# A diffusion layer on one core: the values' copies out of PSUM placed behind a weight block's split, and a small transpose one step of products later

## The chip, the core and the metric

The kernel runs on one core of one Trainium2 chip. The metric is the device time of one execution in microseconds (us); the number given for a kernel is the median of its runs. Five engines run side by side, each through its own queue and in the order of that queue: TensorE (PE in the profile, with its weight loads as PEld), VectorE (DVE), ScalarE (ACT), GpSimd (POOL) and SyncE (SP), which here issues the DMA transfers. Semaphores order the engines against each other.

## The reference

One layer of a diffusion backbone in float32, with 256 latent tokens, 256 context tokens and 2048 channels. Both kinds of token are normed and modulated (a scale and a shift that come from a conditioning vector, different for latent and context tokens). The result h is multiplied by one large matrix for queries, keys, values and gates:

```
h  = rms_norm(x, g) * (1 + scale)   + shift
hc = rms_norm(ctx, g) * (1 + scale_c) + shift_c
qa, ka, va, qb, kb, vb, ga, gb = split(h @ w_in)
```

Two attentions follow (a windowed one with 8 query heads and 2 key heads, and one over a neighbourhood with 8 heads; both also see the context), then gates, two branch matrices, an output matrix, and a gated feed-forward part with a short convolution. The values that this case is about are va and vb: 512 tokens by 10 heads of 128 channels, 1280 columns in all.

## The kernel before

**Numbers and splits.** Float32 products are made of two parts: each operand is split into a high part and the rest (names ending in h and l), and each product is three matmuls: high by high, low by high, high by low. A weight block of 128 x 2048 numbers is loaded by SyncE into one of four buffers called `raw`; ScalarE writes its high part `wh` (line 144) and VectorE the rest `wl` (line 148), in two halves of 1024 columns each. There are two buffers of `wh` and two of `wl`, so a block can be split when TensorE has read the block two before it for the last time.

**The stages.** By the first and last start of their matmuls in the trace: modulation and keys (`pk`) to 148.8 us, the values (`pv`) from 149.1 to 264.8, queries and attention (`pq`) to 426.6, gates and branches (`pg`, `pb`) to 677.8, the output matrix (`py_o`) to 764.7, the feed-forward matrix up (`pu`) to 1261.5 and down (`c`, `x`) to 1490.4.

**The values.** Lines 738 to 765 compute them in three column groups: 512, 512 and 256 columns wide, with 4, 4 and 2 weight blocks. The document counts these blocks from 0 to 9 (`nb` in the code): 0 to 3 are group 0, 4 to 7 group 1, 8 and 9 group 2; block 10 is the first one of the queries. A group accumulates in four PSUM banks, one for each 128 tokens (`pv0_0` to `pv0_3` for group 0 and so on). Six banks take turns for such sums: group 2's first two are free for a long time when it begins, its third and fourth are those of group 1's first and second. When a group's products are through, ScalarE copies the four banks into `vv` (line 765).

A block is walked in steps (`kk`): four steps for a wide group, eight for the narrow one, with four token tiles of three matmuls in each. The call `block(2)` at a block's beginning asks for the split of the next block and for the load of the one after it. `last` holds the two instructions of the latest split; `last[0]` is ScalarE's.

**What goes on beside them.** The keys were multiplied before the shift was known, so what the shift adds is computed during the value products. `late_dots` and `shift_done` (lines 675 to 693) finish the shift on VectorE and add it to the last channels of h. `shift_rows` (line 695) subtracts the two shifts (line 696, into `rim`), transposes the columns of the shift to rows on TensorE (`ptsd`, line 698), copies them out on ScalarE (line 700), sends them to memory and brings them back spread over all partitions (`shr`, lines 701 to 704). `beside` (line 718) then lets VectorE take one dot product of 2048 columns (line 726) for each head of keys against that row, out of a `raw` buffer that it loads too; `kb` is the sum, and `key_bias` (line 709) adds it to `kT` on ScalarE (line 712), with a rotation by position (`tr_k`, lines 319 to 322) for the last two heads. While no keys are due, `beside` takes dot products of a later modulation instead (line 247).

**What sets the order.** In this part of the program a scheduler places the instructions of each engine, led by the order of the code and its own estimates. `tc.issue_after(x)` binds the instructions inside it to stand behind x on x's engine. So the code says what must be computed and the scheduler says in which order; the order of instructions that it gives is shown below.

## Time and profile before

| | |
|---|---|
| median of 3 runs | 1501.37 us (1500.74 to 1503.16) |
| the profiled execution | 1499.85 us |
| its span in the profile | 1498.1 us |
| granted clock of TensorE, mean | 0.999 |
| TensorE busy | 1483.5 us (99%) |
| VectorE busy | 1220.7 us (81%) |
| ScalarE busy | 820.0 us (55%) |

The span runs from the first to the last instruction that the profiler saw; the execution's own time has 1.75 us more around it. In a timeline, a row has the start in us from the span's beginning, the duration, the engine, the line, the operation, what it writes and reads, how many instructions the row takes together and, in brackets, how long the engine stood idle before and what ended that. In a list of waits, a row says which instruction waited for which engine's instruction, for how long in total, how many times, and the longest.

### The profile page before, as it was taken

The numbers are of one execution on the slowest core, as the hardware profiler recorded it, in microseconds if no ns is written. First come the engines' busy times: TensorE is split into PE (matmuls) and PEld (weight loads), VectorE is DVE, ScalarE is ACT, GpSimd is POOL, SyncE is SP. The second block draws the span as 40 slices with busy tenths as digits, with TensorE's granted clock in tenths as the row PEclk, the third lists the DMA queues.
The fourth block names the chain that finished last, engine by engine and source line by source line (L and its number), as shares of the span: only waits on it lengthen the run. The fifth ranks groups of instructions, "written<-read, shape, count | busy, mean of one in ns | idle before, by whom it ended". The sixth has DMA issues, their size and how long they took to land.

```text
span 1498.1 us, 21728 instructions
## 1 busy us (share of the span) xinstructions
PE 1483.5 (99%) x8487; PEld 1279.7 (85%) x8487; DVE 1220.7 (81%) x1852; ACT 820.0 (55%) x1361; POOL 1.8 (0%) x11
## 2 busy tenths in 40 slices
PE   9999999999999999999999999999999999999998
PEld 7877888998988888888888888888888888888886
DVE  4499877889988888877778887887888878887887
ACT  5553323677765445555666555555555556445543
POOL 0000000000000000000000000000000000000000
PEclk9999999999999999999999999999999999999999
DMA  9988696764468888878856666666666654655652
GB/s 372 396 320 338 262 399 256 298 213 158 152 225 299 311 320 328 314 273 336 317 201 223 251 231 242 237 240 231 249 222 231 225 186 166 225 219 187 263 216 112
DMA packets 61159, 383.72 MB, mean 256 GB/s; under 512 B 6512, under 2 KB 8960, under 8 KB 18304
## 3 DMA queue, kind: packets, MB, share of 16 engines
q1 hardware_dynamic: 60336, 381.26, 68.1%
q8 instruction: 67, 1.10, 0.3%
q10 hardware_dynamic: 720, 1.07, 0.2%
q14 instruction: 36, 0.29, 0.1%
HBM read 378.05 MB, written 4.25 MB: 255 GB/s over the span
## 4 chain that ended last, share of the span: by engine, by line
PE 95%; DVE 2%; ACT 1%; issue 1%; DMA 1%; POOL 0%; SPq 0%; DVEq 0%; POOLq 0%
PE pu L217 21%; PE c L1368 12%; PE pu L218 11%; PE pg L217 7%; PE pk L498 7%; PE py_o L993 6%; PE pv L760 5%; PE pq L217 4%; PE pb L217 4%; PE pg L218 4%; PE x L1368 3%; PE pq L218 2%; PE pb L218 2%; PE po L901 1%; PE s L870 1%; PE pm L371 1%
## 5 line engine op out<-in xcount | busy, mean ns | idle before, releaser
L148 DVE TENSOR_TENSOR wl<-raw,wh 128x1024 fp32r<-128x1024 f32 (+1 forms) x444 | 521.2, 1202 | 134.4 <-ACT wh L144 133.5
L144 ACT ACTIVATE wh<-raw 128x1024 fp32r<-128x1024 f32 (+1 forms) x444 | 444.6, 1037 | 201.2 <-PE pg L217 54.8
L217 PE MATMUL pu<-h,wh 128*128 128x512 f32 x1404 | 487.6, 391 | 0.0
L218 PE MATMUL pu<-h,wl 128*128 128x256 f32 x1404 | 396.0, 282 | 0.0
L217 PEld LDWEIGHTS pu<-h,wh 128*128 128x128 f32 x1404 | 263.6, 188 | 54.7
L218 PEld LDWEIGHTS pu<-h,wl 128*128 128x128 f32 x1404 | 265.7, 189 | 0.0
L217 PE MATMUL pg<-h,wh 128*128 128x512 f32 x464 | 161.5, 390 | 0.0
L1368 PE MATMUL c<-wh,ff 128*128 128x512 f32 x448 | 138.0, 389 | 0.0
L218 PE MATMUL pg<-h,wl 128*128 128x256 f32 x464 | 130.9, 282 | 0.0
L498 PE MATMUL pk<-h,ku 128*128 128x512 f32 x480 | 117.6, 398 | 0.5 <-DVE h L412 0.3
L222 ACT ACTIVATE half_u<-pu 128x256 f32<-128x256 f32 x88 | 33.5, 383 | 147.9 <-PE pu L218 147.9
L247 DVE SCALAR_TENSOR_TENSOR raw<-raw,crb 128x2048 f32<-128x2048 f32 x48 | 109.6, 2286 | 2.8 <-DMA raw<-in_wm_b_dram 2.8
L217 PE MATMUL pq<-h,wh 128*128 128x512 f32 x304 | 108.8, 396 | 2.3 <-ACT wh L144 2.3
L498 PEld LDWEIGHTS pk<-h,ku 128*128 128x128 f32 x480 | 87.7, 188 | 24.0 <-issue 3.9
L217 PEld LDWEIGHTS pg<-h,wh 128*128 128x128 f32 x464 | 87.1, 188 | 18.1
L760 PE MATMUL pv<-wh,h 128*128 128x512 f32 (+1 forms) x384 | 101.3, 354 | 1.2 <-ACT wh L144 1.2
L1368 PEld LDWEIGHTS c<-wh,ff 128*128 128x128 f32 x448 | 84.1, 188 | 17.4
L217 PE MATMUL pb<-h,wh 128*128 128x512 f32 x256 | 89.4, 391 | 0.0
L218 PEld LDWEIGHTS pg<-h,wl 128*128 128x128 f32 x464 | 87.8, 189 | 0.0
L1368 PE MATMUL c<-wl,ff 128*128 128x512 f32 x224 | 87.4, 390 | 0.0
L218 PE MATMUL pq<-h,wl 128*128 128x256 f32 x304 | 85.6, 282 | 0.0
L993 PE MATMUL py_o<-wh,zz 128*128 128x512 f32 x256 | 78.4, 389 | 0.0
(252 smaller groups left out, 2090.6 us busy)
## 6 DMA issues: line engine op xcount, KB each, us to landing
raw<-in_ws_dram SPq DMA_DIRECT2D x222, 1024.0 KB, 4.9
raw<-in_wm_b_dram SPq DMA_DIRECT2D x64, 1024.0 KB, 4.9
raw<-in_wm_sc_dram SPq DMA_DIRECT2D x15, 1024.0 KB, 8.2
raw<-in_wkt_dram SPq DMA_DIRECT2D x10, 1024.0 KB, 7.5
raw<-in_wm_sh_dram SPq DMA_DIRECT2D x8, 1024.0 KB, 9.3
sd<-in_wm_sd_dram SPq DMA_DIRECT2D x6, 1024.0 KB, 6.2
raw<-in_wk_dram SPq DMA_DIRECT2D x7, 768.0 KB, 8.4
crb<-sild SPq DMA_DIRECT2D x5, 1024.0 KB, 8.7
```

Source lines behind the costliest of these rows:

```text
L144: a_ = nc.scalar.activation(hi, src, AF.Copy)
L148: v_ = nc.vector.tensor_tensor(out=lo, in0=src, in1=hi, op=ALU.subtract)
L217: nc.tensor.matmul(pt[:, :], wh[:, w], a, start=first and i == 0, stop=False, skip_group_check=True)
L218: nc.tensor.matmul(pt[:, :S], wl[:, w], a[:, 0], start=False, stop=last and i == n - 1, skip_group_check=True)
L222: a_ = nc.scalar.activation(t[:], pt[:, S:], AF.Copy)
L247: nc.vector.scalar_tensor_tensor(out=r, in0=r, scalar=1.0, in1=row, op0=ALU.mult, op1=ALU.mult, accum_out=modx[:, j : j + 1])
L371: nc.tensor.matmul(pm[32 * j : 32 * j + 32, t * P : t * P + P], cc[:, q, :], rsc[k + t][:, q * P : q * P + P], start=q < 4, stop=q >= KT - ...
L498: nc.tensor.matmul(pk[:], wt[:, w], hh[:, :, k, a], start=k == 0 and a == 0 and wt is wh, stop=k == KT - 1 and a == 1)
L760: nc.tensor.matmul(pv[i][:, :nw], src[:, k, a, t0 : t0 + P], wt[:, w], start=k == 0 and q == 0, stop=k == KT - 1 and q == 2)
L870: nc.tensor.matmul(s_ps, qs[hd][:, a, qt * P : qt * P + P], k_[:, w], start=q == 0, stop=q == 2)
L993: p_ = nc.tensor.matmul(py[t][:], act[:, k, a, t * P : t * P + P], wt[:, w], start=k == 0 and q == 0, stop=k == nk - 1 and q == 2)
L1368: nc.tensor.matmul(pt[:], a(i), wt[:, w], start=k not in begun, stop=stop and q == 2, skip_group_check=True)
```

## The change

Two edits. The four copies of a group (line 765) are put into `tc.issue_after(last[0])`, so that on ScalarE they stand behind the high part of the block whose split was asked for last; at the end of a group that is the first block of the next one. And the call of `shift_rows` in block 2 comes at step 3 instead of step 2. No instruction is added or taken away, and no operand changes. Lines behind the first edit have a number that is higher by one.

```diff
-                        if (nb, kk) == (2, 2):
+                        if (nb, kk) == (2, 3):
                             shift_rows()
...
                     nb += 1
-                for i in range(4):
-                    nc.scalar.activation(vv[:, i, n0 : n0 + nw], pv[i][:, :nw], AF.Copy)
+                with tc.issue_after(last[0]):
+                    for i in range(4):
+                        nc.scalar.activation(vv[:, i, n0 : n0 + nw], pv[i][:, :nw], AF.Copy)
```

The order of ScalarE's instructions at the border of groups 1 and 2, before (-) and after (+). `pv_0_1780` to `pv_3_1783` are group 1's four banks, `wh_1988` is block 8, the first of group 2; `kT` is the keys' addition for three heads.

```order
-L712 ACTIVATE kT<-kT,kb 128x256 x2
-L765 ACTIVATE vv<-pv_0_1780 128x512
-L765 ACTIVATE vv<-pv_1_1781 128x512
-L712 ACTIVATE kT<-kT,kb 128x256
-L765 ACTIVATE vv<-pv_2_1782 128x512
+L712 ACTIVATE kT<-kT,kb 128x256 x3
 L144 ACTIVATE wh_1988<-raw_1927 128x1024 x2
-L765 ACTIVATE vv<-pv_3_1783 128x512
+L766 ACTIVATE vv<-pv_0_1780 128x512
+L766 ACTIVATE vv<-pv_1_1781 128x512
+L766 ACTIVATE vv<-pv_2_1782 128x512
+L766 ACTIVATE vv<-pv_3_1783 128x512
```

Three copies stood ahead of the block's split and now stand behind it, as the fourth did; the third of the `kT` steps is now ahead of all of them. At the end of group 0 and of group 2 the copies stood behind the next block's split before, and nothing moves there.

TensorE's order at the first product of group 2: `pv_0_2070` to `pv_3_2073` are its four banks, `wh_1988` and `wl_1989` block 8. What an instruction waits for is in brackets.

```order
 L760 MATMUL pv_1_2071<-wh_1988,h 128x256 x2
-L760 MATMUL pv_2_2072<-wh_1988,h 128x256 x2
-L760 MATMUL pv_3_2073<-wh_1988,h 128x256 x2
 L760 MATMUL pv_0_2070<-wl_1989,h 128x256 [waits DVE_49]
 L760 MATMUL pv_1_2071<-wl_1989,h 128x256
+L760 MATMUL pv_2_2072<-wh_1988,h 128x256 [waits Activation_49]
+L760 MATMUL pv_2_2072<-wh_1988,h 128x256
 L760 MATMUL pv_2_2072<-wl_1989,h 128x256
+L760 MATMUL pv_0_2070<-wh_1988,h 128x256
+L760 MATMUL pv_3_2073<-wh_1988,h 128x256 [waits Activation_49]
+L760 MATMUL pv_3_2073<-wh_1988,h 128x256
 L760 MATMUL pv_3_2073<-wl_1989,h 128x256
```

The products of the third and fourth bank come later by a few matmuls, and each now has a wait of its own for ScalarE, since these banks were group 1's.

TensorE's order around the transpose of the shift: `ptsd` is that transpose, `rim` the shift's columns, `wl_1564` block 2.

```order
 L760 MATMUL pv_3_1512<-wh_1563,h 128x512 x2
+L760 MATMUL pv_3_1512<-wl_1564,h 128x512
 L698 MATMUL ptsd<-ident,rim 48x128 [waits DVE_49]
-L760 MATMUL pv_3_1512<-wl_1564,h 128x512
 L760 MATMUL pv_0_1509<-wh_1563,h 128x512 x2
```

The transpose stands one matmul later. On VectorE and SyncE no instruction changes its place.

## The prediction

> **What bounds the kernel now.** I read the page first, then the waits of the matmul engine, then the timeline of the value products on each engine.

> The page: share of the span, busy tenths of VectorE (DVE) in 40 slices of 37 us, and the costliest group.

> ```profile
> span 1498.1 us, 21728 instructions
> PE 1483.5 (99%) x8487; PEld 1279.7 (85%) x8487; DVE 1220.7 (81%) x1852; ACT 820.0 (55%) x1361; POOL 1.8 (0%) x11
> DVE  4499877889988888877778887887888878887887
> L148 DVE TENSOR_TENSOR wl<-raw,wh 128x1024 fp32r<-128x1024 f32 (+1 forms) x444 | 521.2, 1202 | 134.4 <-ACT wh L144 133.5
> ```

> TensorE (PE) is busy for 1483.5 of 1498.1 us, so a change that leaves its work alone can win only from the 14.6 us in which it is idle. The waits of PE over the whole span (total, times, longest), less two of 0.3 and 0.2 us among the keys ahead of them:

> ```profile
> PE pq L217 <- ACT wh L144: 2.3, 1, 2.3
> PE busy L279 <- POOL ident masks.py:199: 1.9, 1, 1.9
> PE pv L760 <- ACT wh L144: 1.2, 1, 1.2
> PE ptsd L698 <- DVE rim L696: 0.8, 1, 0.8
> ...
> PE s L870 <- ACT h L144: 0.2, 1, 0.2
> ...
> ```

> Three of the four largest, 2.3, 1.2 and 0.8 us, lie among the value products. The timeline of PE shows them (start, duration, idle before). First the shift's row, then the border between group 1 (blocks 4 to 7, 512 columns) and group 2 (blocks 8 and 9, 256 columns), then that between blocks 8 and 9.

> ```profile
> 178.31 0.61 PE L760 MATMUL pv<-wh,h 128*128 128x512 f32 x2
> 179.74 0.29 PE L698 MATMUL ptsd<-ident,rim 128*48 128x128 f32 x1 [0.82 <-DVE rim L696]
> ...
> 236.80 0.39 PE L760 MATMUL pv<-wh,h 128*128 128x512 f32 x1
> 237.03 0.39 PE L760 MATMUL pv<-wl,h 128*128 128x512 f32 x1
> 238.57 1.21 PE L760 MATMUL pv<-wh,h 128*128 128x256 f32 x8 [1.16 <-ACT wh L144]
> 239.83 0.39 PE L760 MATMUL pv<-wl,h 128*128 128x256 f32 x1
> ...
> 240.40 0.40 PE L760 MATMUL pv<-wh,h 128*128 128x256 f32 x2
> 240.64 0.28 PE L760 MATMUL pv<-wl,h 128*128 128x256 f32 x1
> ...
> 250.48 1.12 PE L760 MATMUL pv<-wh,h 128*128 128x256 f32 x8
> 253.85 0.49 PE L217 MATMUL pq<-h,wh 128*128 128x512 f32 x1 [2.25 <-ACT wh L144]
> 254.28 0.50 PE L760 MATMUL pv<-wl,h 128*128 128x256 f32 x2
> ```

> Matmuls overlap, so the loss is read from starts. A 512-column one follows another after 0.23 us (236.80 to 237.03), so after 237.03 the next was due at 237.26; it came at 238.57, 1.31 us late. A 256-column one takes 0.28 and follows after 0.12 (two from 240.40 to 240.64). The last of the eight starts at 238.57 + 1.21 - 0.28 = 239.50, the next was due at 239.62 and came at 239.83: 0.21 more. First stall: 1.52 us. Likewise the last of block 9's first eight starts at 250.48 + 1.12 - 0.28 = 251.32, pq was due at 251.44 and came at 253.85 (2.41 late), and wl, due 0.23 behind it, at 254.28 (0.20). Second stall: 2.61 us.

> Why was the weight block late? ScalarE (ACT), which makes wh, in the same stretch:

> ```profile
> 235.41 1.28 ACT L765 ACTIVATE vv<-pv 128x512 f32<-128x512 f32 x2 [9.22 <-PE pv L760]
> 236.59 0.50 ACT L712 ACTIVATE kT<-kT,kb 128x256 f32<-128x256 f32 x1
> 236.98 0.59 ACT L765 ACTIVATE vv<-pv 128x512 f32<-128x512 f32 x1
> 237.46 2.01 ACT L144 ACTIVATE wh<-raw 128x1024 fp32r<-128x1024 f32 x2
> ...
> 249.99 0.91 ACT L712 ACTIVATE kT<-kT,kb 128x256 f32<-128x256 f32 x2 [2.14 <-DVE kb L730]
> 250.80 1.05 ACT L144 ACTIVATE wh<-raw 128x1024 fp32r<-128x1024 f32 x1
> 251.87 0.84 ACT L319 ACTIVATE tr_k<-kT 64x256 f32<-64x256 f32 x2
> 252.74 1.06 ACT L144 ACTIVATE wh<-raw 128x1024 fp32r<-128x1024 f32 x1
> ```

> ACT stands idle for 9.22 us in front of a copy that only PE's last products release, with block 8's split queued behind it until 237.46. DVE stands behind that split:

> ```profile
> 228.00 0.08 DVE L726 DVE_READ_ACCUMULATOR raw<-raw,shr 128x1 f32 x1
> 238.55 2.36 DVE L148 TENSOR_TENSOR wl<-raw,wh 128x1024 fp32r<-128x1024 f32 x2 [10.47 <-ACT wh L144]
> 240.83 2.29 DVE L726 SCALAR_TENSOR_TENSOR raw<-raw,shr 128x2048 f32<-128x2048 f32 x1
> ...
> 249.80 0.15 DVE L730 TENSOR_TENSOR kb<-kb 128x1 f32<-128x1 f32 x1
> ...
> 253.00 1.23 DVE L148 TENSOR_TENSOR wl<-raw,wh 128x1024 fp32r<-128x1024 f32 x1
> ```

> So the second stall is the child of the first: DVE's 10.47 us make kb late (249.80), kT waits for it, and behind kT stand tr_k and the split at 252.74 for which pq waits.

> **The change, part by part.** The copies. By the order of instructions (shown above), only ACT's order at the border of groups 1 and 2 changes: block 8's two split instructions pass three copies, and the third kT step passes two. At the other two borders the copies stood behind the split already, and nothing is moved there. Nothing is added, DVE and SyncE keep their order, no DMA moves. Whether block 8 can be split early depends on three things: the third kT step, its load, and a free wh buffer. SyncE's queue with the loads (start of the issue, number issued):

> ```profile
> 221.25 0.33 SPq L137 DMA_DIRECT2D raw<-in_ws_dram  x1
> 223.46 4.97 SPq L137 DMA_DIRECT2D raw<-in_wkt_dram  x3
> 240.94 2.54 SPq L137 DMA_DIRECT2D raw<-in_ws_dram  x2
> ```

> What these took to land, in the view of the transfers (the first row for the load issued at 221.25, the second for the last of the three):

> ```profile
> raw<-in_ws_dram SPq DMA_DIRECT2D x1, 1024.0 KB, 6.9
> raw<-in_wkt_dram SPq DMA_DIRECT2D x1, 1024.0 KB, 7.5
> ```

> The load of block 8 was issued at 221.25 and landed 6.9 us later, at 228.15. Its buffer was block 6's; block 7 has 48 products of 0.23 us, 11.0 in all, before 237.26, so block 6 ended at about 226.3. The third kT step (in the trace at 236.59, for 0.50 us) takes the sum that DVE reads out until 228.08: the split can start at 228.6, 8.8 us earlier, and ends at 230.6, well ahead of the first copy at 235.41. The copies then start when they did; the one that came behind the split moves forward. PE finds wh and wl ready at 237.26. Its products for the third and fourth bank wait for the first and second copy, done by 236.7, while PE reaches them after 237.9: no wait. Term 1: -1.52 us; its cover is the 4.8 us between 230.6 and 235.41, and without it the old stall comes back.

> DVE's chain moves with the split: wl from 229.7, the key dot products from 232.0 (their three loads were issued from 223.46 to about 228.1 and land 7.5 us after at most, the last at 235.6, needed at 238.7). kb comes 8.8 us earlier, at 241.0, tr_k ends at about 244, the first half of block 9's wl starts at 244.2, and the next blocks are loaded from 232.1 instead of from 240.94. What is late next is the buffer: block 10's split takes block 8's, which is free when the last product that reads it ends. That one starts 0.24 us before block 9's eight (its wl product lies between) and takes 0.28, so it ends 0.04 us after their start; with 0.06 for the signal (the subtraction below ends at 179.68, PE starts at 179.74) ACT begins 0.1 us after their start, at 250.48 - 1.7 + 0.1 = 248.9. From there the half split takes 1.11 us until pq can start (252.74 to 253.85) while the eight take 0.96: a wait of 0.1 + 1.11 - 0.96 = 0.25 us stays. Term 2: -(2.61 - 0.25) = -2.4 us. Bounds: 0 if another instruction holds ACT, 2.6 if the wait goes whole.

> The shift's row. PE's order shows the transpose moved by one matmul only; the scheduler had pulled it ahead. DVE's subtraction, which releases it, stays where it is:

> ```profile
> 179.51 0.17 DVE L696 TENSOR_TENSOR rim<-rim 128x16 f32<-128x16 f32 x1
> ```

> It ends at 179.68, PE takes the transpose at 179.74 in either order, but has done one product of 0.23 us more by then. The copy of the transposed row and its three DMAs keep their places on ACT and SyncE. Term 3: -0.2 us, between 0 and the whole delay: the next product was due at 178.31 + 0.46 = 178.77, and the transpose came 0.97 later.

> The sum. 1.5 + 2.4 + 0.2 = 4.1 us. The profiled execution took 1499.85 us with a span of 1498.1; it lies 1.5 below the median of 1501.37, and I take the gain off the median: 1497.3 us. Behind the value products PE's only listed wait is 0.2 us, ahead of the scores (s): loads, splits and sums start when PE frees a buffer, so all moves forward together.

> In the rows, the copies' own start is set by PE at 235.41, in either order. [...]

> **The rivals.** "Only the first stall goes" (12 in 100). Term 2 needs kb by about 246.1: in the trace the late split started 2.8 us after kb was ready, and it is wanted at 248.9. If loads or DVE take up over 5 of the 8.8 us, pq still waits. Against: the three key loads have their landing recorded. Gain 1.5 + 0.2: 1499.6 us.

> "The gain is given back" (10 in 100). DVE runs at 8 tenths and more nearly throughout; if it were the true pace later, PE would only wait elsewhere. Against: its largest idle, 133.5 us, is for ACT's wh, which waits for buffers that PE frees, and PE lists no wait for DVE behind the value products. Time: 1501.4.

> "The split is late and the copies hang behind it" (5 in 100). If block 8's load or buffer is ready only after 235.41, the copies wait with the split, and PE for both. A split at 237.46 costs what it costs now; each us beyond adds one. The landings of the weight loads between 219 and 262 us, least, median, most:

> ```profile
> DMA to landing us min/median/max: 4.8/6.4/7.8
> ```

> Even the slowest would land at 229.1. With a split at 240.0 it would be 2.5 us slower, 1503.9 us.

> **How the numbers follow.** My forecast has 70 in 100; 3 are left for what I don't see. The low end: all three stalls gone whole (1.52 + 2.61 + 0.97 = 5.1) give 1496.3, and the lowest run lies 0.6 under the median: 1495.7. The high end takes in the first rival, 1499.6, and 1.2, half of the runs' spread of 2.4: 1500.8; the other two rivals and part of the rest, under 20 in 100, stay out. 0.2%, about what a measurement can tell from no change, is 3.0 us, only 1.1 us less than the forecast's gain, and the runs scatter by that much: I give the forecast five chances in six to pass it, 0.58 in all. Slower is the third rival, 0.05; the rest, 0.37, is the same.

> **What would show it.** Right: ACT's wh split of block 8 at about 228.6 in front of the first copy; the wait "PE pv <- ACT wh" gone from the list; "PE pq <- ACT wh" down to 0.1 to 0.4; DVE's idle of 10.47 down to about 1.5; the transpose's wait at about 0.6; the stages behind 4 us earlier. Wrong: PE waits for a copy (vv) or wl at the border, the split starts after 232, or a new wait of PE behind 265 us. A span reduced by less than 3 us though both stalls are gone would say that the gain is given back.

## The result, and the profile after

| | before | after |
|---|---|---|
| median | 1501.37 us (1500.74 to 1504.09, 9 runs) | 1496.63 us (1494.98 to 1498.88, 9 runs) |
| the profiled execution | 1499.85 us | 1498.88 us |
| its span | 1498.1 us | 1497.1 us |

The ratio of the times is 0.9967, with a 95% interval of 0.9957 to 0.9978: the change gains 4.7 us, between 3.3 and 6.5. The two profiled executions differ by 1.0 us only, so the profile has to say two things: where the gain came, and what this one execution lost elsewhere.

The list of TensorE's waits in the changed kernel (total, times, longest). Both waits for `wh`, of 2.3 and 1.2 us, are gone; the wait of the transpose has grown from 0.8 to 2.2 us.

```profile
PE ptsd L698 <- DVE rim L696: 2.2, 1, 2.2
PE busy L279 <- POOL ident masks.py:199: 1.9, 1, 1.9
PE pm L371 <- DMA raw<-in_wm_sc_dram: 0.6, 2, 0.4
...
PE s L871 <- ACT h L144: 0.2, 1, 0.2
```

ScalarE's timeline at the border of groups 1 and 2, and at block 10's split (start, duration; the copies are line 766 now):

```profile
232.17 0.51 ACT L712 ACTIVATE kT<-kT,kb 128x256 f32<-128x256 f32 x1 [1.99 <-DVE raw L726]
232.58 2.00 ACT L144 ACTIVATE wh<-raw 128x1024 fp32r<-128x1024 f32 x2
238.46 2.64 ACT L766 ACTIVATE vv<-pv 128x512 f32<-128x512 f32 x4 [3.88 <-PE pv L760]
...
245.10 0.91 ACT L712 ACTIVATE kT<-kT,kb 128x256 f32<-128x256 f32 x2 [0.44 <-DVE kb L730]
...
251.90 1.06 ACT L144 ACTIVATE wh<-raw 128x1024 fp32r<-128x1024 f32 x1 [4.06 <-PE pv L760]
```

Block 8's split (232.58) stands in front of all four copies and ends 3.88 us before the first of them can start. And the split for which `pq` waits is no longer held up by a late `kb`: at 251.90 what releases it is PE's last product out of the buffer. VectorE in the same stretch, with an idle time of 1.53 us where there were 10.47:

```profile
233.66 2.36 DVE L148 TENSOR_TENSOR wl<-raw,wh 128x1024 fp32r<-128x1024 f32 x2 [1.53 <-ACT wh L144]
...
244.91 0.15 DVE L730 TENSOR_TENSOR kb<-kb 128x1 f32<-128x1 f32 x1
```

On TensorE, at both borders:

```profile
240.08 0.39 PE L760 MATMUL pv<-wl,h 128*128 128x512 f32 x1
240.30 0.64 PE L760 MATMUL pv<-wh,h 128*128 128x256 f32 x4
240.78 0.40 PE L760 MATMUL pv<-wl,h 128*128 128x256 f32 x2
...
251.82 1.12 PE L760 MATMUL pv<-wh,h 128*128 128x256 f32 x8
253.01 0.50 PE L217 MATMUL pq<-h,wh 128*128 128x512 f32 x1
253.34 0.64 PE L760 MATMUL pv<-wl,h 128*128 128x256 f32 x4
```

The first stall is gone whole: group 2 starts 0.22 us behind group 1's last product, and `wl` follows without a gap. At the second, the last of the eight starts at 251.82 + 1.12 - 0.28 = 252.66, so `pq` was due at 252.78 and comes 0.23 late; `wl`, due at 253.24, comes 0.10 late. The two stalls cost 4.13 us before and cost 0.33 now: 3.8 us less.

What ate most of that in this execution lies some 60 us ahead of the first stall. The shift's transpose, on TensorE, and the granted clock (the last figure but two of a row of the windows) behind it:

```profile
178.84 0.39 PE L760 MATMUL pv<-wl,h 128*128 128x512 f32 x1
181.42 0.29 PE L698 MATMUL ptsd<-ident,rim 128*48 128x128 f32 x1 [2.19 <-DVE rim L696]
...
183.16 1.05 PE L760 MATMUL pv<-wh,h 128*128 128x512 f32 x2
184.01 0.63 PE L760 MATMUL pv<-wl,h 128*128 128x512 f32 x1
...
186.36 0.39 PE L760 MATMUL pv<-wl,h 128*128 128x512 f32 x1
```

```profile
182.00:184.00 2.00, 2.00 (x7) 1.55 (x6) 2.00 (x4) 0.93 (x3) 0.00 (x0) 0.67 1.09 377
184.00:186.00 2.00, 2.00 (x6) 1.60 (x5) 2.00 (x5) 0.42 (x1) 0.00 (x0) 0.50 0.94 380
186.00:188.00 2.00, 2.00 (x10) 1.60 (x10) 2.00 (x3) 1.59 (x2) 0.00 (x0) 0.98 0.94 374
```

The product behind 178.84 was due at 179.07, the transpose came at 181.42: 2.35 us lost, against 0.97 before. And PE is called busy in each window, yet the first two count 7 and 6 matmuls in 2 us and the third, nearly at full clock, 10: the granted clock is half. The three rows lack 0.33, 0.50 and 0.02 of full clock over 2 us each, 1.7 us in all, which is half clock for 3.4 us. The 14 matmuls that start between 181.47 and 186.36 take 4.89 us instead of 14 x 0.227 = 3.18: 1.7 us more. So -3.8 + (2.35 - 0.97) + 1.7 = -0.7, of the -1.0 measured.

### The profile page after: what moved, and what is told of

It is laid out like the page before. It is cut to its first block, busy times and chain, and to the rows that moved or that the text cites. A ratio compares the mean times of both kernels' runs of the same rounds, so it can differ in the third digit from the quotient of the medians.

```text
span 1497.1 us, 21728 instructions
## 1 busy us (share of the span) xinstructions
PE 1483.9 (99%) x8487; PEld 1279.7 (85%) x8487; DVE 1220.8 (82%) x1852; ACT 820.5 (55%) x1361; POOL 1.8 (0%) x11
## 4 chain that ended last, share of the span: by engine, by line
PE 96%; DVE 2%; DMA 1%; issue 1%; ACT 1%; SPq 0%; DVEq 0%
PE pu L217 21%; PE c L1369 12%; PE pu L218 11%; PE pg L217 7%; PE pk L498 7%; PE pv L760 6%; PE py_o L994 6%; PE pq L217 4%; PE pb L217 4%; PE pg L218 4%; PE x L1369 3%; PE pq L218 2%; PE pb L218 2%; PE po L902 1%; PE s L871 1%; PE pt L893 1%
## 5 line engine op out<-in xcount | busy, mean ns | idle before, releaser
L148 DVE TENSOR_TENSOR wl<-raw,wh 128x1024 fp32r<-128x1024 f32 (+1 forms) x444 | 520.9, 1201 | 131.3 <-ACT wh L144 130.5
L144 ACT ACTIVATE wh<-raw 128x1024 fp32r<-128x1024 f32 (+1 forms) x444 | 444.7, 1036 | 207.0 <-PE pg L217 54.8
L217 PE MATMUL pu<-h,wh 128*128 128x512 f32 x1404 | 487.6, 390 | 0.0
L217 PEld LDWEIGHTS pu<-h,wh 128*128 128x128 f32 x1404 | 263.4, 188 | 55.0
L217 PE MATMUL pg<-h,wh 128*128 128x512 f32 x464 | 161.5, 390 | 0.0
L217 PE MATMUL pq<-h,wh 128*128 128x512 f32 x304 | 108.8, 396 | 0.1
L760 PE MATMUL pv<-wh,h 128*128 128x512 f32 (+1 forms) x384 | 102.7, 357 | 0.0
L217 PEld LDWEIGHTS pg<-h,wh 128*128 128x128 f32 x464 | 87.1, 188 | 18.2
L217 PE MATMUL pb<-h,wh 128*128 128x512 f32 x256 | 89.4, 390 | 0.0
## 6 DMA issues: line engine op xcount, KB each, us to landing
raw<-in_ws_dram SPq DMA_DIRECT2D x222, 1024.0 KB, 4.9
raw<-in_wm_b_dram SPq DMA_DIRECT2D x64, 1024.0 KB, 4.9
raw<-in_wm_sc_dram SPq DMA_DIRECT2D x15, 1024.0 KB, 8.2
raw<-in_wkt_dram SPq DMA_DIRECT2D x10, 1024.0 KB, 7.6
raw<-in_wm_sh_dram SPq DMA_DIRECT2D x8, 1024.0 KB, 9.3
sd<-in_wm_sd_dram SPq DMA_DIRECT2D x6, 1024.0 KB, 6.2
crb<-sild SPq DMA_DIRECT2D x5, 1024.0 KB, 9.4
```

The source lines that it names most:

```text
L144: a_ = nc.scalar.activation(hi, src, AF.Copy)
L148: v_ = nc.vector.tensor_tensor(out=lo, in0=src, in1=hi, op=ALU.subtract)
L217: nc.tensor.matmul(pt[:, :], wh[:, w], a, start=first and i == 0, stop=False, skip_group_check=True)
L760: nc.tensor.matmul(pv[i][:, :nw], src[:, k, a, t0 : t0 + P], wt[:, w], start=k == 0 and q == 0, stop=k == KT - 1 and q == 2)
```

## The experiments

Three theories stood at the start. A: the gain is the two stalls, gone because block 8 is split early; the transpose's wait differs from execution to execution, and the clock falls where it is long. B: moving the transpose brings part of the gain. C: the gain comes from elsewhere, or is scatter. In each short diff the lines are those of the kernel that the text names.

**Each edit alone.** First the changed kernel without the transpose's move:

```diff
-                        if (nb, kk) == (2, 3):
+                        if (nb, kk) == (2, 2):
```

> Only the copies' edit; the transpose stays one matmul earlier, as before. Theory A (the gain is the two stalls that the late split of block 8 causes): both waits for wh at 238.6 and 253.9 us are gone and the time is 3.8 us under before (the two stalls of 1.52 and 2.61 less the 0.33 us that stay in front of pq), about 1497.6; 0.2 us slower than the whole change, which can't be told apart. Theory B (the transpose's move gives the 0.6 to 0.9 us that the change gained beyond my sum): 3.0 to 3.8 us under before and clearly 0.7 us or more behind the whole change.

Measured: 1496.53 us (1495.23 to 1497.17, 5 runs), the kernel before on the same chip 1501.28 (1498.65 to 1505.12, 21 runs): ratio 0.9968, 0.9955 to 0.9980. The copies alone bring the gain of the whole change, as far as the intervals can tell. The transpose's wait in its profile is 0.8 us, and the granted clock behind it stays at 1.00.

Then the kernel before with the transpose's move alone (2, 2 to 2, 3):

> Only the transpose's move by one matmul; the copies stand as before. Theory A: both waits for wh stay (1.2 and 2.3 us in the list of waits), and the time is that of before less 0.2 us, within the noise (ratio 0.9985 to 1.0010). Theory B: 0.7 to 1 us faster than before.

Measured: 1502.34 us (1499.57 to 1504.29, 11 runs), ratio 1.0004, 0.9995 to 1.0013. Theory B falls: this edit by itself moves nothing that can be measured; by the interval it gains 0.8 us at most. Both waits for `wh` are there as before (2.3 and 1.2 us), and the transpose waits 1.8 us.

**The transpose behind the whole of block 2.** With the call at (2, 3) the scheduler still pulls the transpose ahead, to a place where PE waits for it. So it was bound to the last matmul of block 2, 12 matmuls (2.7 us) further back; this also puts the row's way to memory and back (`shd`, `shr`) behind one more load in SyncE's queue. In the changed kernel, and with the same edit in the kernel before:

```diff
-            def shift_rows():
+            def shift_rows(after):
...
-                nc.tensor.transpose(pt[: 3 * KT, :P], rim[:, : 3 * KT], ident[:])
+                with tc.issue_after(after):
+                    nc.tensor.transpose(pt[: 3 * KT, :P], rim[:, : 3 * KT], ident[:])
...
-                        if (nb, kk) == (2, 3):
-                            shift_rows()
+                        if (nb, kk) == (3, 0):
+                            shift_rows(mm.ins)
...
-                                nc.tensor.matmul(
+                                mm = nc.tensor.matmul(
```

> The whole change, and the transpose bound to stand four steps' worth less, one step further back: in front of block 3 instead of block 2's last step, 2.7 us later on TensorE. Theory A (TensorE stands in front of the transpose for 0.8 to 2.2 us, differently in each execution, and loses more when its clock drops after the longer waits): the wait for rim is gone from the list, the granted clock is 1.00 from 180 to 190 us in every execution, the time is 1 to 2 us under the whole change (1494.6 to 1495.8), and the runs scatter by less than 2 us instead of 3.9. Theory C (the scatter and the rest of the gain come from elsewhere): the time is at most 1.0 us under the whole change and the scatter stays at 3 to 4 us.

Measured in the changed kernel: 1494.90 us (1494.81 to 1497.33, 5 runs), ratio 0.9958, 0.9945 to 0.9972. No wait of the transpose, and a granted clock of 1.00 from 178 to 190 and from 232 to 260 us. The runs scatter by 2.5 us, more than theory A allowed; one run in five makes it so, and it is taken up below.

> The kernel before with nothing but the transpose bound one step further back, in front of block 3. Theory A: 1 to 2 us faster than before, the two waits for wh unchanged (1.2 and 2.3 us). Theory C: no more than 1.0 us, and the scatter of before (3.4 us) stays.

Measured in the kernel before: 1500.58 us (1498.92 to 1501.40, 11 runs), ratio 0.9991, 0.9982 to 1.0000. The wait is gone there too, but the gain can't be sized: 0.7 us by the medians, 1.4 by the ratio, between 0 and 2.7 by its interval, so neither theory is ruled out here. Its profile showed something else, a granted clock of 0.83 and 0.74 in two windows of 4 us (252 to 260) that begin at the second stall. The profile of the transpose's move alone showed the same (0.84 and 0.73), that of the kernel before on which the prediction rests none.

**How early must the split be?** In the changed kernel, block 8's split was put behind the first copy, so that, counted from the start of group 1's last product, it starts about one us earlier than before the change instead of seven or eight:

```diff
-                    wh, wl = block(2)
+                    wh, wl = block(2, nb != 7)
...
+                def copy(i):
+                    return nc.scalar.activation(vv[:, i, n0 : n0 + nw], pv[i][:, :nw], AF.Copy).ins
+
+                if c == 1:
+                    first = copy(0)
+                    queue[b0 + 8] = (first, first)
+                    split_to(b0 + 8)
                 with tc.issue_after(last[0]):
-                    for i in range(4):
-                        nc.scalar.activation(vv[:, i, n0 : n0 + nw], pv[i][:, :nw], AF.Copy)
+                    for i in range(1 if c == 1 else 0, 4):
+                        copy(i)
```

> The changed kernel, but block 8's split stands behind the first copy of group 1 on ScalarE, and the other three copies behind the split. So the split starts at about 236.3 to 236.5 us instead of 228.6, one or two us earlier than in the kernel before (237.46), and its high part is there 1 us earlier. Theory A (the second stall is the child of VectorE's late chain, and needs the split some 5 us earlier): the first stall shrinks from 1.5 to 0.2 to 0.7 us, the second stays at 2.0 to 2.6 us in the waits of TensorE, and the time is 1499.5 to 1500.7 us against 1501.3 of the kernel before. Rival (any order in which the first copies don't hold the split up is enough, and the second stall goes with the first): both waits for wh fall under 0.5 us and the time is 1496.5 to 1497.5 us, as with the whole change.

Measured: 1499.86 us (1498.66 to 1503.07, 11 runs), the kernel before on the same chip 1501.89 (1499.85 to 1504.09, 21 runs): ratio 0.9989, 0.9980 to 0.9998. Its ScalarE and TensorE:

```profile
237.14 0.60 ACT L765 ACTIVATE vv<-pv 128x512 f32<-128x512 f32 x1 [6.91 <-PE pv L760]
...
238.03 2.00 ACT L144 ACTIVATE wh<-raw 128x1024 fp32r<-128x1024 f32 x2
```

```profile
238.75 0.39 PE L760 MATMUL pv<-wl,h 128*128 128x512 f32 x1
239.14 0.98 PE L760 MATMUL pv<-wh,h 128*128 128x256 f32 x6
240.40 0.62 PE L760 MATMUL pv<-wl,h 128*128 128x256 f32 x3 [0.28 <-DVE wl L148]
...
254.42 0.49 PE L217 MATMUL pq<-h,wh 128*128 128x512 f32 x1 [2.00 <-ACT wh L144]
```

The first stall is down from 1.52 to 0.60 us (239.14 was due at 238.98, and `wl` at 239.96), the second is still there with 2.00 us idle. So the second doesn't vanish with the first. Against the start of group 1's last product, the split starts 0.43 us late in the kernel before (237.46 to 237.03), 0.72 early here (238.03 to 238.75) and 7.50 early in the changed kernel (232.58 to 240.08), where VectorE gets its block in time and the second stall goes, as theory A has it. How early is enough, between one us and seven, was not tried.

**Does a long wait halve the clock?** The changed kernel with one more VectorE multiplication in front of the shift's sums; its result isn't used. Where the scheduler would have moved other work, instructions were bound to their places, which the diff leaves out:

```diff
-                            shift_done()
+                            with tc.issue_after(last[1]):
+                                x_ = nc.vector.tensor_tensor(out=junk[:], in0=crb[0][:], in1=crow_c[:], op=ALU.mult)
+                            with tc.issue_after(x_.ins):
+                                shift_done()
```

> The changed kernel with one more VectorE multiplication of 128x2048 (about 2.3 us, its result isn't used) ahead of the sums of the shift, so that the transpose of the shift's row waits 2.3 us longer; the order of ScalarE and SyncE is that of the changed kernel. Theory A (TensorE's granted clock falls to half for some 4 us when it has waited over about 2 us, which costs 1.7 us more): the transpose's wait is 3.0 to 4.5 us, the granted clock in the 4 to 6 us behind it is near 0.5 in the profile, and the time is 2.3 us over the changed kernel plus up to 1.7: 1499 to 1500.6 us. Rival (the half clock seen in the profile of the changed kernel had another cause): the granted clock stays at 1.00 behind the longer wait, and the time is 2.3 us over the changed kernel, 1498.9 us or less.

Measured: 1499.57 us (1497.40 to 1500.94, 11 runs), ratio 0.9983, 0.9974 to 0.9992; the changed kernel in the same comparison took 1497.10. By the time alone the two theories can't be told apart, since the interval reaches over 1498.9 on both sides. The profile tells them: TensorE's row, and its windows.

```profile
182.81 0.29 PE L705 MATMUL ptsd<-ident,rim 128*48 128x128 f32 x1 [3.59 <-DVE rim L701]
```

```profile
182.00:184.00 2.00, 1.19 (x4) 0.99 (x5) 1.97 (x5) 1.56 (x4) 0.00 (x0) 0.78 0.99 406
184.00:186.00 2.00, 2.00 (x6) 1.55 (x5) 2.00 (x5) 0.31 (x2) 0.00 (x0) 0.50 0.42 168
186.00:188.00 2.00, 2.00 (x9) 1.58 (x9) 2.00 (x3) 0.70 (x1) 0.00 (x0) 0.87 0.87 283
```

A wait of 3.59 us, and half clock for 3.4 us behind it (0.22, 0.50 and 0.13 of full clock are lacking over 2 us each), in the profiled execution.

**The changed kernel again, and beside it the late transpose again** (no edit, and the same as above):

> The changed kernel once more, as the neighbour of the two others and of the next. Theory A: 1496.0 to 1497.2 us in the median, with a scatter of 2 to 4 us, and a wait of the transpose between 0.8 and 2.3 us in the profile, with the granted clock under 1 behind it only where the wait is near 2. Rival (the profile taken first was typical): a wait near 2.2 us and the half clock again.

> The changed kernel with the transpose behind all products of block 2, once more, to see whether it beats the changed kernel on the same chip. Theory A (the transpose's wait of 0.8 to 2.2 us and the clock behind it are all that is left there): 1494.8 to 1495.5 us, 1 to 2 us under the changed kernel, no wait of the transpose, and a scatter under 1 us in most runs. Rival (the difference of the first comparison was scatter): within 0.5 us of the changed kernel.

Measured: the changed kernel 1497.10 us (1496.53 to 1497.57, 5 runs; ratio 0.9969, 0.9956 to 0.9981), with the late transpose 1494.85 (1494.57 to 1495.88, 5 runs; ratio 0.9955, 0.9943 to 0.9968). In this comparison the two don't overlap, and 2.2 us lie between them; in the first one it was 1.7 against the 9 runs shown at the top, and one run of five lay higher, in whose profile the values start 2.8 us later than in the second (151.62 against 148.84), as TensorE is slower in the first 15 us: the first nine key products take 4.19 us there and 2.73 here. The fifteen key products from 16.44 us on there and from 13.68 on here take 3.88 and 3.85 us. Why the start was slow was not shown. The version with the late transpose is the best of the study. The second profile of the changed kernel shows a transpose that waits less, and no fall of the clock (1.00 in all windows of 2 us from 180 to 190). The runs of the changed kernel scatter by 1.0 us here, less than the 2 to 4 that were expected:

```profile
178.74 0.39 PE L760 MATMUL pv<-wl,h 128*128 128x512 f32 x1
180.67 0.29 PE L698 MATMUL ptsd<-ident,rim 128*48 128x128 f32 x1 [1.54 <-DVE rim L696]
...
249.48 1.12 PE L760 MATMUL pv<-wh,h 128*128 128x256 f32 x8
250.67 0.50 PE L217 MATMUL pq<-h,wh 128*128 128x512 f32 x1
```

**The kernel before, profiled three more times**, without an edit, for the clock behind its second stall:

> The kernel before, unchanged, for its profile: how often is its second stall followed by a drop of TensorE's granted clock? Theory A (an idle time of TensorE of about 2.2 us is at the edge: in some executions the clock falls to half for some 4 us, which costs 1.7 us, and this is why the change gained more than the stalls alone): in the three looks together at least one with the second stall at 2.2 us or more shows a granted clock under 0.8 in one of the windows of 2 us behind it, and its queries' products start later than those of the others by some 1.7 us. Rival (the half clock behind the second stall belongs to the edits of the experiments): 1.00 in all looks.

> A second look at the kernel before, with the expectations of the first.

> A third look at the kernel before, with the expectations of the first.

Measured: 1502.69, 1502.67 and 1502.59 us in the three profiled executions; one more run of the same kernel beside them, without a profile, took 1505.09. All three show the half clock (0.50, 0.56 and 0.50 in the lowest window of 2 us). The first of them, on TensorE and by windows:

```profile
251.51 1.12 PE L760 MATMUL pv<-wh,h 128*128 128x256 f32 x8
254.88 0.49 PE L217 MATMUL pq<-h,wh 128*128 128x512 f32 x1 [2.24 <-ACT wh L144]
...
267.32 0.28 PE L760 MATMUL pv<-wl,h 128*128 128x256 f32 x1
```

```profile
256.00:258.00 2.00, 2.00 (x12) 2.00 (x11) 2.00 (x4) 0.17 (x1) 0.45 (x2) 0.50 0.78 324
258.00:260.00 2.00, 2.00 (x13) 2.00 (x13) 2.00 (x3) 0.00 (x0) 0.00 (x0) 0.67 0.73 217
260.00:262.00 2.00, 2.00 (x19) 2.00 (x18) 2.00 (x2) 0.00 (x0) 0.00 (x0) 1.00 1.02 385
```

From `pq` to the last value product it takes 267.32 - 254.88 = 12.44 us here. The profile on which the prediction rested has the same products between 253.85 and 264.81, in 10.96 us: 1.5 us less, at full clock.

**One account of all of them.** For each profiled execution, what TensorE lost at the transpose, at the two stalls, and to the half clock behind either, all read from starts as above:

| execution | time | transpose late | first stall | second stall | half clock | time less these |
|---|---|---|---|---|---|---|
| before, of the prediction | 1499.85 | 0.97 | 1.52 | 2.61 | 0 | 1494.8 |
| before, first of the three | 1502.69 | 1.88 | 1.52 | 2.60 | 1.48 | 1495.2 |
| split behind the first copy | 1500.40 | 1.92 | 0.60 | 2.35 | 0 | 1495.5 |
| long wait | 1500.31 | 3.75 | 0 | 0.35 | 1.70 | 1494.5 |
| after, first profile | 1498.88 | 2.35 | 0 | 0.33 | 1.70 | 1494.5 |
| after, second profile | 1496.60 | 1.70 | 0 | 0.34 | 0 | 1494.6 |
| copies alone | 1496.02 | 0.95 | 0 | 0.34 | 0 | 1494.7 |
| late transpose, second profile | 1494.57 | 0 | 0 | 0.34 | 0 | 1494.2 |

Eight executions that differ by 8 us come out within 1.3 us of each other: the stalls, the transpose's wait and the clock behind them are nearly all of it. The five that are not in the table, read in the same way, come out at about 1494.9 (the transpose's move alone), 1495.2 and 1495.1 (before, second and third of the three), 1495.7 (before with the late transpose) and 1497.0 (late transpose, first profile). The last one is the exception: its 2 us more go with the slow first 15 us told above. Theory A holds for the gain; what is left for C is such a start of the kernel, which the change does not touch.

## Why the prediction was right, step by step

**Term 1, the first stall, 1.52 us.** Right, gone whole in every profile of the changed kernel. The split came later than the forecast's 228.6, at 232.58 in one profile and 231.41 in the other, since VectorE's dot products and block 8's load were later too (in the first profile the third sum is read out until 232.13 us instead of 228.08, and the load is issued at 224.56 instead of 221.25), and in the first profile all of TensorE's products: group 1's last one starts at 240.08 instead of 237.03. So the sign of being wrong "the split starts after 232" came true there without meaning what it was to mean; counted from that product the split was 7.5 us ahead. Its cover, forecast at 4.8 us, was 3.9 and 2.7, and was not used up.

**Term 2, the second stall, -2.4 us.** The mechanism was right, and the wait that it leaves was right to 0.02 us: `kb` at 244.91 instead of 249.80, later than the 241.0 of the forecast but ahead of the 246.1 that was needed; the split set free by the buffer, 0.08 us after the eight products begin (251.82 to 251.90), `pq` 1.11 us after that, and 0.23 us of wait left where 0.25 was forecast. The rival by which only the first stall goes did not come; the split behind the first copy shows what it would have looked like.

**What the second stall costs was too small.** The prediction read the stall's price as lost starts, 2.61 us, from an execution in which the clock stayed up. So the term is mis-sized by a cost that the prediction put at nothing. In the three other profiles of the kernel before, and in both variants that keep the stall whole, TensorE ran at half clock behind it and lost 1.3 to 1.5 us more. That makes 3.8 + 1.5 us where the clock falls, and 3.8 where it doesn't; 4.7 us, the difference of the medians, lies between the two. It also goes some way to explain why the profiled execution lay 1.5 us under the median, a gap that the prediction set aside; its transpose was also late by only 0.97 us, against 1.9 to 2.1 in the three others. The runs without a profile agree: a fall, half clock for 3.41 us, takes 1.7 of 1498 us, 0.001, off a run's mean clock, and of the 42 runs of the kernel before in the two comparisons above, the 26 with a mean clock of 0.998 or less have a median of 1502.3 us and the 16 with 0.999 one of 1500.9. This is a hint and no proof, as the mean also holds the half clock at the kernel's end, which lasts 3.1 us of the span in the prediction's execution and 3.7 in the changed kernel's first profile.

**Term 3, the transpose, -0.2 us.** This step failed: that the subtraction which releases the transpose "stays where it is" holds for the order, not for the time. It stands 11.64 us behind the first dot product that reads the broadcasts of the modulation (`crb`), in each of these four profiles, and that one's start moves with their landing from execution to execution: with a median of 7.2 us from issue to landing the subtraction starts at 179.64 (copies alone), with 7.9 at 179.51 (before, where the issue was 0.8 us earlier), with 8.4 at 180.44 (after, second profile), with 9.1 at 181.19 (after, first profile). One product more in front of it is worth 0.23 us in that scatter; the transpose's delay was 0.95 to 2.1 us in five profiles of the old order and 1.70 to 2.35 in four of the new, and the edit alone showed no effect. The "about 0.6" for its wait was met nowhere.

**The sum and the rivals.** 4.1 us were forecast, 4.7 (3.3 to 6.5) came. The 0.6 us over lie within the interval; the clock behind the second stall is enough to account for them, and Term 3 brought nothing. That the total came so near is in part luck, as a term too large and a term too small stand in it. "The gain is given back" did not happen: in the first of the three new profiles of the kernel before, the feed-forward matrix's products (`pu`) run from 775.3 to 1264.1 us, in the changed kernel's second profile from 769.1 to 1257.9, 6.2 us earlier at both ends. In the two profiles of the result they run from 772.5 to 1261.3 and from 771.5 to 1260.3, 1.0 us earlier at both ends. That is the other sign that misled: a span reduced by less than 3 us with both stalls gone was to say that the gain is given back later, and here the rest was lost earlier, at the transpose and in the clock behind it. "The split is late and the copies hang" did not happen either. The copies waited for PE in either order (ScalarE stood idle for 9.22 us in front of the first one before, for 3.88 in the changed kernel), and group 2 did not wait for its banks: no row of PE's waits names a copy.

## What to carry to other kernels

An instruction that waits for TensorE's last product holds up everything behind it in its engine's queue (here ScalarE stood idle for 9.22 us with the split behind it); if that is the split of the next block, put the split in front, and look one stage on, since the late engine hands its delay to the next border (here VectorE's 10.47 us of idle time led to the second stall, 2.61 us). Price a stall of TensorE from several executions, and read the granted clock for some us behind it: here the second stall, with an idle time of 2.24 to 2.26 us, cost half as much again (1.3 to 1.5 us) in five executions and nothing more in the sixth, so that one profile could miss it. Where a wait hangs on a DMA's landing, put work of the landing's scatter in front (the medians from issue to landing lay between 7.2 and 9.1 us), not one product (0.23 us).

## What the runs showed of the hardware

The traces also show where 2.25 and 2.25 differ. In the changed kernel's first profile the recorded clock is full from 5.18 us, half from 182.67, full from 186.08 and half from 1493.39; in the prediction's execution it is full from 6.77 and half from 1494.98. Counted from the start of the full clock, the changes come after 177.49, 180.90 and 1488.21 us in the one and after 1488.21 in the other: 52, 53 and 436 times 3.4133. A grid of that step is an estimate from these four changes. The windows below are two steps each, first in the prediction's execution, the 72nd and 73rd behind 6.77 us, then in the first of the three others, the one ahead of the fall at 255.90 and the one behind it. The figure behind the comma is PE's busy time:

```profile
249.11:252.53 3.42, 2.49 (x21) 2.28 (x20) 3.42 (x7) 2.51 (x5) 0.00 (x0) 1.00 0.71 297
252.53:255.94 3.41, 2.09 (x15) 1.85 (x16) 3.32 (x7) 2.59 (x4) 0.45 (x2) 1.00 0.66 223
```

```profile
252.49:255.90 3.41, 1.17 (x8) 0.79 (x7) 3.32 (x8) 3.35 (x6) 0.00 (x0) 1.00 0.49 151
255.90:259.32 3.42, 3.42 (x19) 3.42 (x18) 3.42 (x5) 0.27 (x1) 0.45 (x2) 0.50 0.75 261
```

By this grid a border cuts the 2.25 us of the prediction's execution into 0.93 and 1.32, and the clock stays up; the 2.24 us of the other lie within a single step, and the clock is half in the next. In all seven executions with a fall, the step ahead of it, counted back from the fall, holds between 1.8 us of idle time (before with the late transpose) and 3.1 (long wait). The waits of the transpose in the first and second of the three, 1.72 and 1.73 us, lie within a single step too, counted back in the same way, and full clock follows. It also follows the waits of 1.77 and 2.00 us with the split behind the first copy, where the borders were not shown. The idle times rest on the profile's modelled ends of matmuls.
